# Within-chunk products of an S5 layer: formed on TensorE from zero-padded coefficients instead of gathered through DRAM

## The chip, the cores and the metric

One of the eight NeuronCores of a Trainium2 chip runs the whole program; the other seven are idle. The metric is device time of one execution in microseconds. Before the change three runs gave 2152.57, 2155.32 and 2158.06 us, median 2155.32. One further execution was profiled; it took 2160.6 us.

## The reference

Two layers of a hybrid encoder in float32, on 256 tokens of width 2048. Layer 0 mixes tokens with a bidirectional diagonal state-space model (S5), layer 1 with windowed attention; each is followed by a squared-ReLU MLP of width 8192. The change concerns the S5 mixer alone:

```
for each direction d (forward, backward), group g of 16 channels (128 groups, 64 states each):
    s[t] = lb[d,g] * s[t -/+ 1] + (f*B)[d,g] u[t]            # complex, over 256 tokens
    y[t] += Re(C[d,g] s[t])
y = y + d_skip * u ;  z = gelu(y)
h = h + (z @ w_glu_a) * sigmoid(z @ w_glu_b)
```

## The kernel before

The 256 tokens are cut into 64 chunks of T = 4. The recurrence runs over chunks only (63 steps); inside a chunk the answer is a product with a 64 x 64 matrix (4 tokens x 16 channels in and out) for each group. The 128 groups are handled in two halves of 64 ("half 0" and "half 1"), and each half in 8 batches of 8 groups, b = 0 to 7. A pair of batches, m = b // 2, shares one tile of products and one PSUM bank of outputs.

For one half the work is:

- `s5_a`: coefficient tables q (L469, VectorE for half 0, GpSimd for half 1), their transposes on TensorE (L477), and the state inputs of all chunks (L449).
- `s5_scan`: the recurrence, 63 steps of three VectorE instructions (L505, L506, L507).
- `s5_expand_steps`: the output tables E of a batch, on GpSimd (four L523 and two L524).
- `s5_kern`: the responses of a batch, B times E, eight matmuls on TensorE (L540), copied out by ScalarE (L547). `finish` adds the skip term on GpSimd (L553) and writes the responses to a DRAM scratch (L554, on SyncE's DMA queue).
- `s5_gather`: two DMAs (L564) read the scratch back with a shifted access pattern, and so form the product tile `tp` of a pair of batches, with zeros where a lag would be outside the chunk.
- `s5_shift`: state copies on ScalarE and VectorE (L582, L583), through a ring of two buffers. `s5_inner`: products times inputs into the output bank (L594). `s5_out`: states times E into the same bank (L607), then gelu. `s5_ztrans`: transposes of gelu's result (L619, L622, L623) into z.

Half 0's z opens the first part of the gated projection, `glu_early`: 32 weight tiles of 512 KB, loaded over ScalarE's queue, split in a high part (L638, ScalarE) and a low part (L639, VectorE or GpSimd), 12 matmuls of 128x512 each (L657 to L659). This work is in `run` placed between and around half 1's steps. The rest of the projection, the MLP, the attention and the second MLP follow; they take the larger part of the time and no step of theirs is edited.

The order on each engine comes from the tile framework's scheduler, which starts from the order of the program and moves instructions by its own estimate; each engine then executes its list strictly in order, and so do the DMA queues of SyncE and ScalarE.

Buffers are places in one arena of SBUF. A tile of half 1 often lies where a tile of half 0 was, so it must wait for that one's last reader: the tables E of half 1's batches 4 and 3 lie where those of half 0's batches 6 and 7 were, and those of batches 0 to 2 where half 0's inputs and states were.

Of the kernel before, what the change touches and what calls it, by code (L numbers as in the profile page):

```python
# [16 lines left out]
P = 128  # L17
# [14 lines left out]
PF = 1  # L32
SB, SC = 10, 2
ER, GM, GL, GA, GC = 0.3, 1, 2, 2, 6
# [132 lines left out]
class Kernel:  # L167
    def __init__(self, ctx, tc, d):
# [4 lines left out]
        self.dram = ctx.enter_context(tc.tile_pool(name="dram", bufs=8, space=bass.MemoryType.DRAM))  # L173
# [101 lines left out]
    def s5_setup(self):  # L275
# [11 lines left out]
        self.msk = ar.get("msk", [16], at=48128)  # L287
        self.dcol = ar.get("dcol", [32], at=48160)
        nc.scalar.dma_start(self.msk, d["dmask"])
        nc.scalar.dma_start(self.dcol, d["dcol"])  # L290
# [141 lines left out]
    def s5_a(self, h):  # L432
# [7 lines left out]
        def statein(b, pin):  # L440
            for i in range(0, 8, 4):
                bk = self.bank()
                for j in range(4):
                    gl = b * 8 + i + j
                    for ri in range(2):
                        for dr in range(2):
                            uu = u[:, gl // 2, gl % 2, :] if dr == 0 else u[:, gl // 2, gl % 2, ::-1]
                            c = (4 * ri + j) * NC
                            pe.matmul(bk[dr * H:(dr + 1) * H, c:c + NC],  # L449
                                      lhsT=pin[:, i + j, ri, dr * H:(dr + 1) * H], rhs=uu, start=True, stop=True)  # L450
# [7 lines left out]
        for b in range(8):  # L458
# [12 lines left out]
            pin = self.r_pin.next()  # L471
            for i in range(0, 8, 2):
                bk = self.bank()
# [4 lines left out]
                po = pin[:, i:i + 2].rearrange("p g r c -> p (g r c)")  # L478
# [4 lines left out]
                yield  # L483
            if prev is not None:
                if b == 1:
                    self.u_trans(h)
                    self.st.append(self.ar.get("st%d" % h, [NC, 2, 64], at=(31744, 23552)[h]))
                statein(*prev)
                yield
# [39 lines left out]
    def s5_kern(self, h, b):  # L529

        nc, d = self.nc, self.d
        g = nc.gpsimd
        u = h * 8 + b
        bp = self.r_bp.next()
        nc.sync.dma_start(bp, d["bp"][u])
        E = self.ex[h, b]
        bk = self.bank()
# [4 lines left out]
        md = self.r_md.next()  # L542
        mb = self.msk.rearrange("p (o c) -> p o c", o=1).broadcast_to([P, 2, 16])
        db = self.dcol[:, u * 2:u * 2 + 2].rearrange("p (g o) -> p g o", o=1).broadcast_to([P, 2, 16])
        g.tensor_mul(md, mb, db)
        kk = self.r_kk.next()
        self.kev = nc.scalar.copy(kk[:, :, 48:176], bk[:, :2 * P].rearrange("p (g c) -> p g c", g=2))  # L547
        if (h, b // 2) not in self.scr:
            self.scr[h, b // 2] = self.dram.tile([32, 4, 2, 448], F32, name="scr")
        scr = self.scr[h, b // 2]  # L550

        def finish():
            self.fin = g.tensor_add(kk[:, :, 48:64], kk[:, :, 48:64], md)  # L553
            nc.sync.dma_start(scr[:, :, b % 2].rearrange("r q c -> q r c"), kk.rearrange("p g c -> p (g c)"))  # L554
        return finish

    def s5_gather(self, h, m, at):

        tp = self.tp[h, m] = self.ar.get("tp%d%d" % (h, m), [16, 64], at=at)
        scr = self.scr[h, m].rearrange("p q x (s c) -> (p q x s) c", c=224)  # L560
        for dr in range(2):
            src = scr[dr * P * 2:(dr + 1) * P * 2, dr * 112:dr * 112 + 64]
            src = bass.AP(tensor=src.tensor, offset=src.offset, ap=[[16, T]] + [list(x) for x in src.ap])
            self.nc.sync.dma_start(tp[dr * 64:dr * 64 + 64].rearrange("p g c -> p (g c)"), src)  # L564

    def s5_kk(self, *ats):

        r = Ring([self.ar.get("kk#%d" % at, [2, 224], at=at) for at in ats])
        for kk in r.tiles:
            self.nc.gpsimd.memset(kk[:, :, 0:48], 0.0)  # L570
            self.nc.gpsimd.memset(kk[:, :, 176:224], 0.0)
        return r
# [12 lines left out]
    def s5_inner(self, h, m):  # L585
# [4 lines left out]
        for x in range(2):  # L590
            for j in range(8):
                i = j % 4 * 4 + x * 2 + j // 4
                c = (x * 4 + j // 2) * 64
                self.nc.tensor.matmul(y[j % 2 * H:(j % 2 + 1) * H, c:c + 64], lhsT=u[:, m * 8 + x * 4 + j // 2, j % 2, :], rhs=tp[:, i],  # L594
                                      start=(x == 0 and j < 2), stop=False, skip_group_check=True)
        self.ar.free("tp%d%d" % (h, m))

    def s5_out(self, h, b):
# [4 lines left out]
        for j in range(0, 8, 2):  # L603
            c = ((b % 2) * 4 + j // 2) * 64
            for n in range(2):
                for r in range(2):
                    pe.matmul(y[r * H:(r + 1) * H, c:c + 64], lhsT=so[:, j + r, n, :], rhs=E[:, j + r, n * T:(n + 1) * T, :], start=False,  # L607
# [539 lines left out]
    def run(self):  # L1147
# [11 lines left out]
        self.ex, self.tp, self.so, self.zt, self.scr, self.ybk = {}, {}, {}, {}, {}, {}  # L1159
        self.r_md = ar.ring("md", 2, [2, 16], at=48192)  # L1160
        self.r_q = ar.ring("q", 2, [8, 3, T, 16], at=4096)
        self.r_pin = ar.ring("pin", 2, [8, 2, P], at=7168)
        self.r_bca = ar.ring("bca", 2, [2, 8, 16], at=11264)
        self.r_bs = ar.ring("bs", 2, [8, 16], at=11776)
        self.r_bc = Ring([ar.get("bc#%d" % at, [2, 8, 2, 16], at=at) for at in (12032, 51712)])
        self.wt = ar.get("wt", [8, T, 16], at=48960)
        self.sct = ar.get("y", [2, 64], at=48704)
# [6 lines left out]
        self.r_bp = Ring([ar.get("bp#%d" % at, [8, 32], at=at) for at in (45568, 45824, 47104, 47360, 47616, 47872)])  # L1174
        self.r_kk = self.s5_kk(46080, 46592, 12544)
# [3 lines left out]
        att = dict(zip(KQ[0], (2048, 3072, 9216, 10240)))  # L1179
# [5 lines left out]
        last = []  # L1185

        def ekern(h, bs, n=0):

            wait = []
            for b in bs:  # L1190
                yield from expand(h, b)
                while last:
                    last.pop()()
                wait = [(m, k - 1) for m, k in wait]
                now = [x for x in wait if x[1] < 0 and (x[0] < 2 or "pin#0" not in ar.live)]
                for m, _ in now:
                    self.s5_gather(h, m, att[m])
                wait = [x for x in wait if x not in now]
                last.append(self.s5_kern(h, b))
                if h == 0 and b % 2:  # L1200
                    wait.append((b // 2, n))
                yield
            if h == 0:
                last.pop()()
                for m, _ in wait:
                    self.s5_gather(h, m, att[m])
        ek = ekern(0, order, 1)
# [3 lines left out]
        interleave(self.s5_a(1), (early(ek, 7 - PF), ER))  # L1211
        ar.free("bca", "bs", "q", "pin", "tab", "bc#12032")
        drain(ek)
        ar.free("kk#12544")
        del self.r_kk.tiles[2:]
        self.r_kk.i = 0
        self.r_bc.tiles[0] = ar.get("bc#12288", [2, 8, 2, 16], at=12288)
        drain(ekern(1, (7, 6, 5)))
        last.pop()()
        ar.free("kk", "bp")  # L1220
# [161 lines left out]
```

## Time and profile before

| | |
|---|---|
| median of three runs | 2155.32 us |
| profiled execution | 2160.6 us, of which its span is 2158.8 us |
| TensorE busy (matmul) | 2012.6 us, 93% |
| VectorE busy | 1247.7 us, 58% |
| ScalarE busy | 994.1 us, 46% |
| GpSimd busy | 337.6 us, 16% |
| mean granted TensorE clock | 0.972 |

The shares are means over very different stages. From 455 us to the end TensorE works almost without a pause; before about 345 us, the S5 mixer, no engine does. The profile page cuts the span into 40 slices, gives busy time by line, and follows back the chain of work that ended last; the trace can be asked for any window. In the rows below, PE is TensorE's matmuls, PEld its weight loads, DVE VectorE, ACT ScalarE, POOL GpSimd, SPq and ACTq the DMA issues of SyncE and ScalarE. An ordinary float32 matmul leaves two records in the trace and a transpose one: the eight matmuls of L540 show as x16.

### The profile page before, as it was taken

How to read it: one execution, taken by the hardware profiler on the slowest of the kernel's cores; microseconds unless marked ns; L12 is line 12 of the kernel's file. 1: busy time of each engine (PE TensorE's matmuls, PEld its weight loads, DVE VectorE, ACT ScalarE, POOL GpSimd, SP SyncE). 2: the span in 40 equal slices, each digit the busy share in tenths (PEclk: the TensorE clock that was granted, in tenths of full speed). 3: DMA queues.
4: the chain of work that ended last, by engine and by line, in shares of the span. 5: the costliest groups of instructions: out<-in, count | busy, mean ns of one | idle time of the engine just before them, and what ended most of it. 6: DMA issues, size and time to landing. Idle time of an engine off the chain costs nothing.

```text
span 2158.8 us, 29177 instructions
## 1 busy us (share of the span) xinstructions
PE 2012.6 (93%) x11860; PEld 1688.9 (78%) x11860; DVE 1247.7 (58%) x1820; ACT 994.1 (46%) x1233; POOL 337.6 (16%) x287
## 2 busy tenths in 40 slices
PE   2945879999999999999999889999999999999999
PEld 2834668878888888888888667788888888888887
DVE  6885924775555554444456777566555555444444
ACT  6734445444444444444444456554444444444442
POOL 6974952110000000000002432020000000000000
PEclk9976989999999999999999999999999999999999
DMA  2233555545555555565554332355555555555554
GB/s 96 59 80 110 174 155 206 184 167 194 187 187 183 192 180 196 193 214 195 201 195 156 127 137 98 118 194 186 195 183 189 195 190 182 202 190 194 194 194 156
DMA packets 78375, 368.49 MB, mean 171 GB/s; under 512 B 23473, under 2 KB 29905, under 8 KB 38305
## 3 DMA queue, kind: packets, MB, share of 16 engines
q1 hardware_dynamic: 72704, 346.78, 47.0%
q10 hardware_dynamic: 5328, 19.49, 2.8%
q8 instruction: 93, 1.52, 0.3%
q0 software_dynamic: 208, 0.36, 0.0%
q14 instruction: 42, 0.34, 0.0%
HBM read 360.83 MB, written 5.77 MB: 170 GB/s over the span
## 4 chain that ended last, share of the span: by engine, by line
PE 78%; DVE 7%; POOL 6%; DMA 5%; ACT 3%; issue 2%; SPq 0%; ACTq 0%; POOLq 0%; DVEq 0%
PE bank L849 32%; PE bank L798 22%; PE bank L799 11%; PE bank L657 3%; PE bank L659 3%; PE bank L658 3%; POOL slot L523 2%; POOL slot L524 1%; DMA scr<-slot 1%; DVE slot L639 1%; POOL slot L469 1%; DMA slot<-in_wge 1%; DVE slot L1014 1%; ACT slot L1010 1%; ACT slot L638 1%
## 5 line engine op out<-in xcount | busy, mean ns | idle before, releaser
L639 DVE TENSOR_TENSOR slot<-slot,slot 128x2048 fp32r<-128x2048 f32 (+1 forms) x321 | 713.2, 2225 | 729.4 <-ACT slot L638 725.5
L638 ACT CAST slot<-slot 128x2048 fp32r<-128x2048 f32 (+2 forms) x357 | 623.4, 1752 | 752.9 <-PE bank L849 364.6
L798 PE MATMUL bank<-slot,slot 128*128 128x512 f32 x2048 | 719.7, 397 | 0.0
L849 PE MATMUL bank<-slot,slot 128*128 128x512 f32 x3072 | 696.7, 389 | 0.0
L849 PEld LDWEIGHTS bank<-slot,slot 128*128 128x128 f32 x3072 | 576.6, 188 | 119.6
L799 PE MATMUL bank<-slot,slot 128*128 128x256 f32 x2048 | 571.7, 279 | 0.0
L798 PEld LDWEIGHTS bank<-slot,slot 128*128 128x128 f32 x2048 | 385.3, 188 | 92.2
L799 PEld LDWEIGHTS bank<-slot,slot 128*128 128x128 f32 x2048 | 386.9, 189 | 0.4
L657 PE MATMUL bank<-slot,slot 128*128 128x512 f32 x544 | 219.8, 405 | 2.3 <-ACT slot L638 1.2
L658 PE MATMUL bank<-slot,slot 128*128 128x512 f32 x544 | 216.4, 398 | 0.0
L659 PE MATMUL bank<-slot,slot 128*128 128x512 f32 x544 | 204.5, 399 | 6.4 <-POOL slot L639 5.4
L659 PEld LDWEIGHTS bank<-slot,slot 128*128 128x128 f32 x544 | 102.6, 191 | 30.1 <-POOL slot L639 6.7
L807 ACT ACTIVATE slot<-slot 128x256 f32<-128x256 f32 x128 | 53.5, 420 | 156.8 <-DVE slot L806 156.8
L657 PEld LDWEIGHTS bank<-slot,slot 128*128 128x128 f32 x544 | 104.9, 193 | 26.4 <-ACT slot L638 1.6
L658 PEld LDWEIGHTS bank<-slot,slot 128*128 128x128 f32 x544 | 104.8, 193 | 21.6 <-issue 0.7
L639 POOL TENSOR_TENSOR slot<-slot,slot 128x1024 fp32r<-128x1024 f32 (+2 forms) x36 | 99.6, 2779 | 99.7 <-ACT slot L638 76.9
L920 POOL DMA_DIRECT2D slot<-in_pos x1 | 0.8, 754 | 611.9 <-DVE slot L842 611.9
L540 PE MATMUL bank<-slot,slot 128*32 128x128 f32 x256 | 13.6, 346 | 54.1 <-POOL slot L524 54.1
L477 PE MATMUL bank<-ident,slot 128*128 128x128 f32 x256 | 42.0, 327 | 21.6 <-DVE slot L469 16.4
L505 DVE TENSOR_TENSOR bank<-bank,slot 128x256 f32<-128x256 f32 x126 | 54.4, 432 | 6.6 <-ACT slot L456 2.4
L806 DVE SCALAR_TENSOR_TENSOR slot<-slot 128x256 f32<-128x256 f32 x128 | 54.2, 425 | 4.2
L477 PEld LDWEIGHTS bank<-ident,slot 128*128 128x128 f32 x256 | 35.8, 169 | 25.7 <-POOL slot L411 16.4
(212 smaller groups left out, 1413.3 us busy)
## 6 DMA issues: line engine op xcount, KB each, us to landing
slot<-in_wup SPq DMA_DIRECT2D x128, 1024.0 KB
slot<-in_wdn SPq DMA_DIRECT2D x128, 1024.0 KB
slot<-in_wqkv SPq DMA_DIRECT2D x20, 1024.0 KB
slot<-in_wge ACTq DMA_DIRECT2D x32, 512.0 KB
slot<-in_wgl SPq DMA_DIRECT2D x16, 1024.0 KB
slot<-in_wo SPq DMA_DIRECT2D x16, 1024.0 KB
slot<-in_cp SPq DMA_DIRECT2D x16, 256.0 KB
slot<-scr SPq DMA_DIRECT2D x16, 256.0 KB
```

The lines of the kernel that those rows point to most:

```text
L477: pe.transpose(bk[:, (2 * j + ri) * P:(2 * j + ri + 1) * P], qf[:, ri * H:ri * H + P], self.ident)
L505: yield v.tensor_mul(xy, lb, st[:, k - 1].rearrange("p r (o g) -> p r o g", o=1).broadcast_to([P, 2, 2, n]))
L638: self.nc.scalar.copy(hi[:, c], raw[:, c])
L639: (self.nc.gpsimd if e == "g" else self.nc.vector).tensor_sub(lo[:, c], raw[:, c], hi[:, c].bitcast(F32))
L657: pe.matmul(out, lhsT=xh, rhs=wh, start=first, stop=False)
L658: pe.matmul(out, lhsT=xl, rhs=wh, start=False, stop=False)
L659: pe.matmul(out, lhsT=xh, rhs=wl, start=False, stop=last)
L798: pe.matmul(bk, lhsT=wh[:, kt], rhs=act[:, kt].rearrange("p x c -> p (x c)"), start=(kt == 0), stop=False)
L799: pe.matmul(bk[:, :L], lhsT=wl[:, kt], rhs=act[:, kt, 0], start=False, stop=(kt == KT - 1))
L806: nc.vector.scalar_tensor_tensor(s, s, 0.0, rb, op0=ALU.max, op1=ALU.mult)
L807: nc.scalar.activation(hT(fb), s, AF.Square)
L849: pe.matmul(bks[tt][cb], lhsT=x[:, ts], rhs=w[:, cb * 512:(cb + 1) * 512], start=(kt == 0 and w is wh and x is hh), stop=(kt == NK - 1 and ...
```

## The change

- The products within chunks are now made by TensorE itself. For a batch, B is stored with 16 zero columns before its 16 real ones (`bz`, 128x672, with the skip coefficients behind), so a 32-column weight slice that starts 16 columns earlier or later lands the 16 real rows in the upper or lower half of a 32-partition quadrant, and adds zeros to the other half. 70 matmuls with 32 weight columns and 16 to 256 moving columns add the responses of the right lags to one PSUM bank; the last four add the skip term. One ScalarE copy of 128x512 puts the bank into `tp`.
- The DRAM scratch, its writes and gathers, the `kk` buffers and their memsets, and the skip term on GpSimd (L545, L553) are gone. The load per batch grows from 128x256 to 128x672 values.
- Half 0's first two `s5_inner` run as soon as their products exist, during `s5_a` of half 1; the other two right after the eighth batch.
- Half 1's tables and products for batches 7, 6, 5 and 4 are placed between half 0's outputs (`EK`), where before 7, 6 and 5 came ahead of all of half 0's outputs; batches 3, 0, 1, 2 follow among the weight tiles of the projection.
- `s5_a`: the transposed tables are in halves of 4 groups in a ring of 3 instead of 8 groups in a ring of 2, and the state inputs of the batch before are issued in the middle of a batch.
- Scan of half 1: `SB, SC` from 10, 2 to 0, 1 (steps issued between half 0's outputs). Some buffers move.

```diff
-SB, SC = 10, 2
-ER, GM, GL, GA, GC = 0.3, 1, 2, 2, 6
+PF, EE, ER = 1, 6, 0.3
+SB, SC = 0, 1
+EK = {1: 7, 3: 6, 5: 5, 6: 4}
+GM, GL, GA, GC = 1, 2, 3, 6
...
-    def s5_kern(self, h, b):
...
-        for j in range(8):
-            q, c = j % 4, j // 4 * P
-            nc.tensor.matmul(bk[q * 32:(q + 1) * 32, c:c + P], lhsT=bp[:, j],
-                             rhs=E[:, j].rearrange("p s c -> p (s c)"), start=True, stop=True)
...
-        def finish():
-            self.fin = g.tensor_add(kk[:, :, 48:64], kk[:, :, 48:64], md)
-            nc.sync.dma_start(scr[:, :, b % 2].rearrange("r q c -> q r c"), kk.rearrange("p g c -> p (g c)"))
-        return finish
-
-    def s5_gather(self, h, m, at):
...
-            self.nc.sync.dma_start(tp[dr * 64:dr * 64 + 64].rearrange("p g c -> p (g c)"), src)
...
+        w = bz[:, :544]
+        sk = bz[:, 544:672].rearrange("p (g c) -> p g c", g=8)
+
+        def mm(q, g, t, lhsT, rhs, start=False, stop=False):
+            self.km = nc.tensor.matmul(o[q * 32:(q + 1) * 32, g, t], lhsT=lhsT, rhs=rhs, start=start, stop=stop, skip_group_check=True)
+        al = slice(0, 8)
+        for q, t in ((0, slice(0, 2)), (3, slice(2, T))):
+            mm(q, al, t, w[:, 512:544], E[:, :, 0:2], start=True)
+        for g in range(8):
+            for k in range(2):
+                for q in range(4):
+                    dr, jj = q // 2, q % 2 * 2 + (k if q % 2 == 0 else 1 - k)
+                    tk = T - 1 - jj
+                    t, lag = (slice(tk, T), slice(0, T - tk)) if dr == 0 else (slice(0, tk + 1), slice(2 * T - 1 - tk, 2 * T))
+                    c = (g * 2 + dr) * 32 + (0 if jj % 2 else 16)
+                    mm(q, g, t, w[:, c:c + 32], E[:, g, lag], start=(g == 0 and k == 0 and q in (1, 2)), stop=(g == 7 and k == 1 and dr == 1))
+        for k in range(2):
+            for q in range(2):
+                tk = T - 1 - (q * 2 + k)
+                c = 0 if k else 16
+                mm(q, al, tk, self.irep[:, c:c + 32], sk, stop=(k == 1))
+        x = b % 2 * 8
+        self.kev = nc.scalar.copy(self.tp[h, m][:, x:x + 8].rearrange("p g c -> p (g c)"), bk)
...
+            if i in EK:
+                drain(expand(1, EK[i]))
+                with self.tc.issue_after(self.om.ins):
+                    self.s5_kern(1, EK[i], att[1][EK[i] // 2])
...
-        for b, m, at in ((4, 3, 50688), (3, 2, 49664), (0, None, 0), (1, None, 0), (2, 0, 2048)):
-            finish = self.s5_kern(1, b)
-            glu(1)
-            finish()
-            if m is not None:
-                self.s5_gather(1, m, at)
+        for b in (3, 0, 1, 2):
+            self.s5_kern(1, b, att[1][b // 2])
             glu(GA)
```

TensorE's list before, from the last state inputs of half 1 to half 0's first outputs (L540 responses of a batch, L594 inner products, L607 outputs, L619 transposes of z; slots are places in the arena, and slot_191 as weights marks half 1's batches here):

```order
L449 MATMUL bank<-slot_85,slot_191 64x64 x64
L540 MATMUL bank<-slot_75,slot_73 32x128 x8
L540 MATMUL bank<-slot_191,slot_73 32x128 x24
L594 MATMUL bank<-slot_75,slot_84 64x64 x19
L607 MATMUL bank<-slot_78,slot_75 64x64 x32
L594 MATMUL bank<-slot_75,slot_84 64x64 x13
L607 MATMUL bank<-slot_87,slot_75 64x64 x16
L619 MATMUL bank<-ident,slot_75 128x128 x4
```

The same place now (L447 state inputs, L544 the new products of a batch, of which the first rows stand here, L583 inner products, L596 outputs, L608 transposes of z):

```order
L447 MATMUL bank<-slot_82,slot_188 64x64 x32
L544 MATMUL bank<-slot_73,slot_79 32x8x32 x2
L544 MATMUL bank<-slot_73,slot_79 32x16
L544 MATMUL bank<-slot_73,slot_79 32x64 x2
...
L544 MATMUL bank<-slot_71,slot_79 32x8x16 x4
L583 MATMUL bank<-slot_188,slot_81 64x64 x32
L596 MATMUL bank<-slot_76,slot_73 64x64 x32
L544 MATMUL bank<-slot_188,slot_79 32x8x32 x2
...
L544 MATMUL bank<-slot_79 32x8x16 x4
L596 MATMUL bank<-slot_84,slot_73 64x64 x16
L608 MATMUL bank<-ident,slot_73 128x128 x4
```

Three batches of half 1 (the x24) stood ahead of half 0's inner products and outputs; now only half 0's last two batches (140 matmuls) stand there, and half 1's batches stand after the first two, the fourth and the sixth output.

SyncE's DMA list before, at half 1's first batches among the projection's weights (in_cp and in_bp are a batch's coefficients, scr the scratch):

```order
L514 DMA slot_191<-in_cp 128x512
L554 DMA scr<-slot_75 4x32x448
L535 DMA slot_191<-in_bp 128x256
L514 DMA slot_86<-in_cp 128x512
L554 DMA scr<-slot_84 4x32x448
L564 DMA slot_86<-scr 64x16x64 x2
L535 DMA slot_191<-in_bp 128x256
L554 DMA scr<-slot_75 4x32x448
L554 DMA scr<-slot_84 4x32x448
```

The last coefficient loads now, up to the projection's second kind of weights (in_wgl):

```order
L534 DMA slot_79<-in_bz 128x672
L534 DMA slot_188<-in_bz 128x672
L534 DMA slot_79<-in_bz 128x672
L514 DMA slot_73<-in_cp 128x512
L514 DMA slot_83<-in_cp 128x512
L534 DMA slot_188<-in_bz 128x672
L534 DMA slot_79<-in_bz 128x672
L514 DMA slot_73<-in_cp 128x512
L534 DMA slot_188<-in_bz 128x672
L622 DMA slot_82<-in_wgl 128x2048 x2
```

Every wait on a scratch write or read has left this queue; what it still waits for is buffers, of which `bz` has five for half 0 and two for half 1.

## Rows read from the trace of the kernel before

**Rows 1.** The profile page, first line.

```profile
span 2158.8 us, 29177 instructions
```

**Rows 2.** Windows: stretch, length; PE, PEld, DVE, ACT, POOL busy; PEclk; DMA share; GB/s.

```profile
79.00:153.00 74.00, 48.78 (x816) 42.70 (x811) 64.61 (x189) 43.64 (x69) 61.21 (x78) 0.84 0.28 74
153.00:181.00 28.00, 3.47 (x54) 2.08 (x56) 8.26 (x15) 0.74 (x2) 20.89 (x23) 0.54 0.35 87
181.00:212.00 31.00, 20.96 (x399) 18.88 (x396) 25.24 (x52) 25.38 (x28) 10.15 (x11) 0.78 0.32 104
212.00:318.00 106.00, 86.11 (x515) 67.23 (x515) 64.45 (x162) 43.39 (x52) 81.35 (x52) 0.89 0.55 161
318.00:345.00 27.00, 27.00 (x339) 22.49 (x337) 10.74 (x11) 17.99 (x19) 9.55 (x4) 0.98 0.66 235
455.00:2158.00 1703.00, 1680.23 (x8605) 1410.76 (x8603) 939.73 (x1199) 764.69 (x934) 82.93 (x43) 0.99 0.52 181
```

**Rows 3.** Chain that ended last, 136 to 185 us: start, length, what.

```profile
172.27 9.01 DMA scr<-slot
...
183.81 1.22 PE bank L607 x17
```

**Rows 4.** The same chain, 264 to 345 us.

```profile
281.94 0.23 PE bank L658
...
291.53 12.83 DMA scr<-slot
...
304.94 10.97 DMA slot<-scr
...
318.03 1.42 PE bank L607 x32
```

**Rows 5.** Waits, 140 to 320 us: who for whom, total us, times, longest.

```profile
ACT slot L547 <- DMA scr<-slot: 20.3, 2, 15.1
POOL slot L523 <- DMA slot<-in_cp: 17.3, 6, 5.5
```

**Rows 6.** Timeline of PE: start, length, line, shape, records merged.

```profile
57.94 1.97 PE L477 MATMUL bank<-ident,slot 128*128 128x128 f32 x16
...
67.66 2.08 PE L449 MATMUL bank<-slot,slot 128*64 128x64 f32 x64
...
79.36 0.64 PE L540 MATMUL bank<-slot,slot 128*32 128x128 f32 x16
...
90.08 3.76 PE L329 MATMUL bank<-ident,slot 128*128 128x128 f32 x32
...
183.81 1.97 PE L607 MATMUL bank<-slot,slot 128*64 128x64 f32 x32 [0.50 <-ACT slot L583]
...
193.26 1.10 PE L594 MATMUL bank<-slot,slot 128*64 128x64 f32 x32
```

**Rows 7.** Window of dense small matmuls, columns as in rows 2.

```profile
60.00:80.00 20.00, 20.00 (x465) 18.79 (x464) 16.32 (x24) 11.74 (x16) 17.30 (x19) 1.00 0.23 62
```

**Rows 8.** Timeline of VectorE: half 0's last step is over, two steps of half 1.

```profile
153.27 0.84 DVE L582 COPY slot<-slot 64x504 f32<-64x504 f32 x1
...
239.25 0.43 DVE L505 TENSOR_TENSOR bank<-bank,slot 128x256 f32<-128x256 f32 x1
...
267.19 0.43 DVE L505 TENSOR_TENSOR bank<-bank,slot 128x256 f32<-128x256 f32 x1
```

**Rows 9.** VectorE by line, 79 to 318 us: count, busy us, mean ns, idle before.

```profile
L639 DVE TENSOR_TENSOR slot<-slot,slot 128x1024 fp32r<-128x1024 f32 x8 | 13.6, 1696 | 1.1 <-ACT slot L638 1.0
L582 DVE COPY slot<-slot 64x504 f32<-64x504 f32 x12 | 10.0, 837 | 48.1 <-PE bank L607 47.8
```

**Rows 10.** GpSimd by line, 0 to 345 us, columns as in rows 9.

```profile
L524 POOL TENSOR_TENSOR slot<-slot,slot 128x512 f32<-128x512 f32 x32 | 44.5, 1391 | 0.5
L523 POOL TENSOR_TENSOR slot<-slot 128x512 f32<-128x512 f32 x32 | 36.6, 1155 | 12.5 <-DMA slot<-in_cp 11.1 <-PE bank L607 1.0
...
L469 POOL TENSOR_TENSOR slot<-slot,slot 128x512 f32<-128x512 f32 x24 | 26.3, 1130 | 0.0
```

More of the change, by code (lines that the diff above doesn't have):

```diff
@@ L470, in s5_a @@
                 yield
-            pin = self.r_pin.next()
+            pin = [self.r_pin.next(), None]
             for i in range(0, 8, 2):
+                if i == 4:
+                    if prev is not None:
+                        if b == 1:
+                            self.u_trans(h)
+                            self.st.append(self.ar.get("st%d" % h, [NC, 2, 64], at=(31744, 23552)[h]))
+                        statein(*prev)
+                        yield
+                    pin[1] = self.r_pin.next()
                 bk = self.bank()
@@ L482, in s5_a @@
                     self.evac = a.copy(po, bk)
[L483 to L488, printed above, removed]
                 yield
@@ L527, in s5_expand, with s5_kern @@
         drain(self.s5_expand_steps(*a))
-    def s5_kern(self, h, b):
[L531 to L535, printed above, removed]
+    def s5_kern(self, h, b, at=None):
+        nc = self.nc
+        u, m = h * 8 + b, b // 2
+        bz = self.r_bz.next()
+        nc.sync.dma_start(bz, self.d["bz"][u])
         E = self.ex[h, b]
+        if (h, m) not in self.tp:
+            self.tp[h, m] = self.ar.get("tp%d%d" % (h, m), [16, 64], at=at)
@@ L1184, in run, with ekern @@
         q = [self.s5_scan(0)]
-        last = []
-        def ekern(h, bs, n=0):
-            wait = []
+        def ekern(h, *bs):
             for b in bs:
                 yield from expand(h, b)
[L1192 to L1201, printed above, removed]
-                yield
[L1203 to L1207, printed above, removed]
+                self.s5_kern(h, b, att[h][b // 2])
+                if b in (1, 3):
+                    self.s5_inner(0, b // 2)
+                yield
+        ek = ekern(0, *order)
         steps(ek, 3 * PF)
@@ L1210, in run @@
         q.append(self.s5_scan(1))
[L1211 to L1212 removed]
+        interleave(self.s5_a(1), (early(ek, EE - PF), ER))
+        ar.free("bca", "bs", "q", "pin", "tab")
         drain(ek)
[L1214 to L1220, printed above, removed]
[L1221 to L1222 removed]
+        ar.free("bc#12032")
+        self.r_bc.tiles[1] = ar.get("bc#6656", [2, 8, 2, 16], at=6656)
+        self.r_bc.i = 1
         def sc(n):
@@ L1231, in run @@
             g.memset(so[:, :, 1, NC - 1:NC], 0.0)
+        for m in range(2, 4):
+            self.s5_inner(0, m)
+        ar.free("bz#45568", "bz#46240", "bz#46912")
+        del self.r_bz.tiles[2:]
+        self.r_bz.i = 0
         prev = None
-        kev = self.kev
         for i, b in enumerate(order):
-            if i % 2 == 0:
-                self.s5_inner(0, b // 2)
-            with self.tc.issue_after(kev.ins):
-                self.s5_shift(0, b, v.tensor_copy)
+            self.s5_shift(0, b, v.tensor_copy)
             self.s5_out(0, b)
```

80 lines of the change are left out of this document (27 added, 53 removed).

## The prediction

> **What bounds the kernel now.** I read the windows first, then the chain, then the waits and single engines. The windows show where TensorE, which carries the program, pauses [rows 2]. From 455 us on it is busy 1680 of 1703 us, and from 318 to 345 us 27 of 27: whatever starts earlier there ends earlier, one for one. Ahead of that it is busy 48.8 of 74 us (79 to 153), 3.5 of 28 (153 to 181), 21.0 of 31 (181 to 212) and 86.1 of 106 (212 to 318): 79.6 of 239 us are idle, and the granted clock falls to 0.54 in the emptiest stretch. The reader should see that no engine is full between 153 and 181 us: VectorE has 8.3 us, ScalarE 0.7, GpSimd 20.9.
>
> The chain says why. At 172.27 a scratch write of 9.0 us ends a wait of ScalarE, whose queue holds the response copies of half 1's batches ahead of half 0's state copies; half 0's outputs start at 183.81 [rows 3], though its recurrence was over at 153.27 [rows 8]. At the other end, 12.8 us of scratch write and 11.0 us of gather follow one another, and half 1's outputs start at 318.03 [rows 4]. The waits show the same queue from two sides: ScalarE's response copy waits 20.3 us for scratch writes, and GpSimd's tables 17.3 us for coefficient loads, which stand behind those writes on SyncE [rows 5].
>
> **The change part by part.** *Scratch, gathers, GpSimd's skip term.* They go, with all waits on them. What is late next is TensorE, because it takes the work over.
>
> *Price of a batch on TensorE.* A batch was eight matmuls, 16 records, 0.64 us [rows 6]. Now it is 70 matmuls, 140 records, 3584 moving columns against 1024. No row shows 16 to 48 moving columns on 32 weight columns. By columns it would be 3.5 x 0.64 = 2.2 us; by records of that row 140 x 0.040 = 5.6 us; by the 64-column records, 2.08 us for 64 and 1.10 for 32, it is 140 x 0.0325 = 4.55 us. At the lower clock the same kind of record took 1.97 / 32 = 0.062 us [rows 6], so 8.6 us a batch. Below 2.2 us I see no reason to go. I take 4.55, as most of the new matmuls have 16 to 64 columns and those rows are nearest, and full clock, because a stretch full of such matmuls was granted 1.00 [rows 7].
>
> What those rows show is about 33 ns a record at 64 columns, whether 64 are needed or fewer. The Trainium skill (TensorEngine Tiling (Array Packing), Instruction Overhead) says that a matmul carries about 60 cycles whatever it streams, so that one column costs as much as 60, and advises against cutting a dimension that is already small. It speaks against this change: as an estimate, 140 times 25 ns is 3.5 us a batch, not 2.2. By the page the sum below would be about 2112 us, by the rows 2125.
>
> *Start of half 0's outputs.* TensorE's list from the end of half 0's state inputs, 79.4 us: half 1's 128 transposes, 1.97 / 16 each, 15.8; its 512 state-input records, 0.0325 each, 16.6; 32 input transposes 3.8; four inner products, 128 records at 0.034, 4.4; eight batches at 4.55, 36.4 [rows 6]. Together 77.0, so 156.4 us without a wait, where before there were 48.8 us of work in 74. VectorE gives nearly the same: its recurrence of half 0 is not touched and ends at 153.3, and four state copies of 0.84 bring it to 156.6 [rows 8, 9]. GpSimd is earlier than both: its eight tables are 8 x (4 x 1.155 + 2 x 1.391) = 59 us and the 24 coefficient products 27 us [rows 10], as before, but without up to 17.3 us of waits. I add 3.5 us for waits of TensorE on tables and on ScalarE's copies: 160 instead of 183.8, **24 us earlier**.
>
> *From there to half 1's first output.* TensorE's list: half 0's 256 output records at 0.034, 8.7; 16 transposes of z, 2.0; 240 weight matmuls at 0.23 [rows 4], 55.2; eight batches, 36.4; half 1's first inner product 1.1. That is 103.4, so 263.4. To this I add 16 us of waits. Eight are for half 0's outputs, which ScalarE paces: 25.4 of 31 us in that stretch before, with TensorE at 21.0 [rows 2]; three new batches fill only part of it. Five are a new wait: the first matmuls of half 1's batch 4 now stand ahead of z's last transposes, and table 4 lies where half 0's table 6 was, so GpSimd can only finish it (about 6 us, two products and two sums left [rows 10]) once half 0's outputs are through. Behind it TensorE's whole list waits, the first weight matmul included. Three are for cold stretches. So 279.4 against 318.0, **38.6 us earlier**, the 24 of the first part among them.
>
> The other engines must allow it. VectorE after 153.3: 63 steps at (267.19 - 239.25) / 25 = 1.118, 70.4; 16 state copies, 13.4; eight low parts, 13.6; with a few us for z it is free at about 254 [rows 8, 9], 25 us before 279. GpSimd: tables 4, 3, 0, 1, 2 from about 188, 37 us, to 225; its first low part belongs to the ninth weight tile, which TensorE reaches after 96 weight matmuls and four to five batches, at about 233.
>
> *Given back.* Counted in the order of TensorE's list, 276 weight matmuls stood ahead of half 1's first output, now 240: 36 x 0.23 = **8.3 us** later.
>
> *Sum.* 38.6 - 8.3 = 30.3. The profiled execution took 2160.6 us (its span of 2158.8 [rows 1] and 1.8 around it), so 2130 for one like it. It lies 5.3 us above the median of the runs, 2155.3; the forecast for the median is **2125 us**.
>
> The regrouped transposes of `s5_a` and the wider coefficient loads I cost at nothing: the former issue the same instructions, the latter are covered by five buffers in half 0. In half 1 there are two, so a load waits for the batch two before it; if that shows, it is the third rival.
>
> **The rivals.** *The price of the small matmuls decides (slower).* TensorE now has nearly no slack, and 16 batches are on its path. Each us of a batch costs up to 16; the gain is gone at 4.55 + 30 / 16 = 6.4 us, 46 ns a record. At the lower clock's 8.6 us the time is 2125 + 16 x 4.05 = 2190. For it: the clock was 0.84 from 79 to 153 and 0.54 afterwards [rows 2], and TensorE waits for each table in list order, which leaves pauses. Against it: those clocks belong to an engine idle for a third of the time and more, and the dense stretch had 1.00 [rows 7].
>
> *Cheaper.* If a record costs 16 to 25 ns, TensorE loses up to 2.3 us x 8 in the second part, but the first stays with VectorE at about 158 and the second cannot pass VectorE's 254 and half 1's state copies: first output at about 262, time 2125 - 17 = 2108. The page's 3.5 us belongs here.
>
> *A new wait on VectorE.* Its list holds 85 instructions of half 1's recurrence, some 28 steps or 31.7 us [rows 8], behind the eighth low part, whose buffer (one of three) is freed by the fifth weight tile's matmuls. I expect that at 214 to 222. If it slips past 247, each us is lost again; 15 late is 2140. For it: in-order lists that cross three engines; against: 25 us of slack.
>
> *The waits change their name only.* Half 0's first products need tables, loads and ScalarE copies in turn; if half 0's outputs still start at about 180, 20 of the 30 us stay away: 2145 to 2155. For it: the recurrences, the tables and ScalarE's copies are untouched. Against it: in the rows of 153 to 181 us only the scratch queue is late.
>
> **How the numbers follow.** Forecast 0.50, for 2113 to 2138 (its own range: 1.6 us a batch less or more in the second part, or half of the waits). Cheaper 0.16, for 2104 to 2113. VectorE's wait 0.10, for 2138 to 2149. Waits renamed 0.14, half of it within 0.3% of 2155.3 (2148.8 to 2161.8, about what a measurement of this kernel can tell from no change) and half below. Slower 0.10, of which 0.03 is within 0.3%. So faster 0.83, same 0.10, slower 0.07. The range that leaves out 2 in 10 is 2106 to 2150: the row price of 5.6 us a batch, 2142, lies in it, the lower clock's price does not.
>
> **What the profile after would show.** No scratch DMA. L544 in 16 groups of 140 records, each 3.5 to 5.6 us long; longer groups make the first rival. Half 0's first L596 at about 160 (153 to 168), half 1's first L596 at about 279 (262 to 292). TensorE over 85% busy from 79 to 153 and at a clock above 0.95. TensorE waiting for GpSimd's table 4 for some us just before the first weight matmul. VectorE's last L507 some 20 us ahead of half 1's first output; if it comes right before it, the third rival holds. The forecast is wrong in its core if half 0's outputs start after 175, or if TensorE's busy time before half 1's outputs grows by over 90 us.

## The result and the profile after

The changed kernel takes 2126.68 us (median of four runs, 2125.68 to 2131.74) against 2156.36 us before: ratio 0.9869, 95% interval 0.9849 to 0.9890, or 29.7 us faster. The forecast was 2125 us. The profiled execution took 2126.57 us (span 2124.8), 34.0 us under the one of before. Eight runs of the changed kernel lie in two groups, four at 2125.7 to 2126.8 and four at 2131.4 to 2131.9 us, whose profiled executions agree up to half 1's last output (299.4 and 299.0 us) and differ in the second MLP, whose first product (L787) takes 356.4 us in one and 362.8 in the other, so differences under 5 us are read from marks in the traces below, not from medians.

The windows after the change, to be laid beside [rows 2] (same columns):

```profile
79.00:153.00 74.00, 63.06 (x1926) 55.20 (x1924) 67.44 (x192) 47.37 (x71) 69.70 (x72) 0.98 0.28 80
153.00:181.00 28.00, 21.51 (x607) 18.27 (x605) 26.14 (x60) 22.47 (x25) 8.43 (x7) 0.70 0.20 65
181.00:212.00 31.00, 24.85 (x424) 19.71 (x417) 29.46 (x60) 6.07 (x9) 26.87 (x20) 0.88 0.47 145
212.00:318.00 106.00, 102.93 (x1158) 82.17 (x1157) 65.22 (x119) 60.31 (x68) 71.24 (x34) 1.00 0.49 163
```

TensorE's idle time from 79 to 318 us falls from 79.7 to 26.7 us, so its busy time grows by 53.0. The empty stretch from 153 to 181 us, 3.5 us of work before, now has 21.5, at a granted clock of 0.70 against 0.54. From 212 to 318 us the clock is 1.00.

TensorE's timeline of the changed kernel at the places the prediction named (start, length, line, shape, records merged, and in brackets the idle time before and what ended it):

```profile
78.47 2.55 PE L544 MATMUL bank<-slot,slot 128*32 128x256 f32 x140
...
151.59 0.34 PE L596 MATMUL bank<-slot,slot 128*64 128x64 f32 x4 [1.99 <-ACT slot L572]
...
157.32 3.58 PE L544 MATMUL bank<-slot,slot 128*32 128x256 f32 x125
...
171.25 0.48 PE L596 MATMUL bank<-slot,slot 128*64 128x64 f32 x4 [4.26 <-DVE slot L572]
...
183.38 1.04 PE L596 MATMUL bank<-slot 128*64 128x64 f32 x28 [0.25 <-DVE slot L573]
188.41 1.14 PE L544 MATMUL bank<-slot,slot 128*32 128x256 f32 x8 [3.99 <-POOL slot L524]
...
192.54 0.78 PE L646 MATMUL bank<-slot,slot 128*128 128x512 f32 x1
...
265.94 1.15 PE L596 MATMUL bank<-slot,slot 128*64 128x64 f32 x31
...
298.24 1.15 PE L596 MATMUL bank<-slot,slot 128*64 128x64 f32 x32
```

A batch of 140 records takes 2.55 us at full clock and about 4.3 at the low one (the row at 157.32 is its first 125 records; the clock granted from 157.3 to 161.5 us was 0.56). Half 0's outputs (L596) run from 151.6 to 184.4 us; there is a wait of 4.26 us for a state copy on VectorE and the foreseen one of 3.99 us for GpSimd's table 4. The first weight matmul (L646) comes at 192.5, half 1's first output at 265.9. The marks in the kernel before, from the same view:

```profile
212.08 0.78 PE L657 MATMUL bank<-slot,slot 128*128 128x512 f32 x1
...
300.21 1.10 PE L607 MATMUL bank<-slot,slot 128*64 128x64 f32 x32
304.19 1.15 PE L607 MATMUL bank<-slot,slot 128*64 128x64 f32 x32
316.05 1.97 PE L594 MATMUL bank<-slot,slot 128*64 128x64 f32 x32 [7.77 <-DMA slot<-scr]
317.79 1.66 PE L607 MATMUL bank<-slot,slot 128*64 128x64 f32 x32
...
341.65 1.15 PE L607 MATMUL bank<-slot,slot 128*64 128x64 f32 x32
```

Here half 1's outputs start at 300.2, not at 318.0: the chain in [rows 4] passes through the third of the eight outputs, the one behind the last gather. With equal marks the gain adds up so (36 weight matmuls fewer stand ahead of half 1's outputs, 36 x 0.228 = 8.2 us):

| mark | before | after | earlier | less the 36 |
|---|---|---|---|---|
| first weight matmul | 212.1 | 192.5 | 19.5 | 19.5 |
| half 1's first output | 300.2 | 265.9 | 34.3 | 26.1 |
| half 1's last output begins | 341.7 | 298.2 | 43.4 | 35.2 |
| end | 2158.8 | 2124.8 | 34.0 | 34.0 |

So I read 19.5 us as the scratch route's waits in half 0 and the pauses around its outputs, 6.6 as waits between there and half 1's outputs, and 9.1 as the wait for the last gather and the records at the lower clock behind it. TensorE's own costliest wait before the change, from 79 to 184 us, names another engine (who for whom, total us, times, longest):

```profile
PE bank L540 <- POOL slot L524: 44.6, 6, 11.5
```

These are GpSimd's tables, which for a part of that time waited for coefficient loads behind the scratch writes [rows 5]. No run takes the scratch route alone out of the kernel before; what the place of the tables is worth without it is the second experiment.

### The profile page after: what moved, and what is told of

Read it like the earlier page. It is cut to its first block, busy times and chain, and to the rows that moved or that the text cites. A ratio compares the mean times of both kernels' runs of the same rounds, so it can differ in the third digit from the quotient of the medians.

```text
span 2124.8 us, 33046 instructions
## 1 busy us (share of the span) xinstructions
PE 2034.0 (96%) x13844; PEld 1706.7 (80%) x13844; DVE 1255.5 (59%) x1820; ACT 996.3 (47%) x1233; POOL 334.5 (16%) x245
## 3 DMA queue, kind: packets, MB, share of 16 engines
q8 instruction: 108, 1.77, 0.3%
## 4 chain that ended last, share of the span: by engine, by line
PE 73%; DVE 4%; ACT 2%; DMA 2%; issue 1%; POOL 0%; SPq 0%; ACTq 0%; DVEq 0%
PE bank L838 32%; PE bank L787 22%; PE bank L788 11%; PE bank L646 2%; PE bank L647 2%; PE bank L648 2%; DVE slot L628 1%; ACT slot L999 1%; DMA slot<-in_wqkv 1%; ACT slot L627 1%; DVE slot L1003 1%; PE bank L1018 1%; PE bank L1009 1%; DVE slot L984 1%; DMA slot<-in_wup 0%
## 5 line engine op out<-in xcount | busy, mean ns | idle before, releaser
L787 PE MATMUL bank<-slot,slot 128*128 128x512 f32 x2048 | 719.5, 397 | 0.0
L787 PEld LDWEIGHTS bank<-slot,slot 128*128 128x128 f32 x2048 | 385.3, 188 | 92.0
L646 PE MATMUL bank<-slot,slot 128*128 128x512 f32 x544 | 218.4, 403 | 6.2 <-ACT slot L627 5.1
L646 PEld LDWEIGHTS bank<-slot,slot 128*128 128x128 f32 x544 | 103.7, 191 | 30.8 <-ACT slot L627 6.5
L483 PE MATMUL bank<-ident,slot 128*128 128x128 f32 x256 | 37.2, 295 | 22.3 <-DVE slot L467 16.0
L664 POOL TENSOR_TENSOR slot<-slot 128x512 f32<-128x512 f32 x16 | 28.9, 1813 | 171.6 <-DVE slot L1117 62.5
L830 ACT CAST slot<-slot 128x256 fp32r<-128x256 f32 x128 | 50.7, 397 | 8.0 <-PE bank L838 7.9
```

What stands on the lines that cost most here:

```text
L646: pe.matmul(out, lhsT=xh, rhs=wh, start=first, stop=False)
L787: pe.matmul(bk, lhsT=wh[:, kt], rhs=act[:, kt].rearrange("p x c -> p (x c)"), start=(kt == 0), stop=False)
L830: nc.scalar.copy(hh, hT(kt))
```

## The experiments

The ratios are to the kernel before, with 95% intervals.

| run | median, us | ratio |
|---|---|---|
| after_again | 2131.60 | 0.9883 (0.9870 to 0.9896) |
| half1_ahead | 2127.08 | 0.9868 (0.9856 to 0.9881) |
| x2_half0 | 2137.16 | 0.9916 (0.9903 to 0.9929) |
| x2_half1_late | 2144.63 | 0.9953 (0.9937 to 0.9970) |
| tables_swapped | 2121.75 | 0.9842 (0.9829 to 0.9855) |
| no_steps_between | 2126.27 | 0.9866 (0.9853 to 0.9880) |
| swap_sc0 | 2127.38 | 0.9874 (0.9857 to 0.9890) |
| scan1_half | 2128.47 | 0.9875 (0.9858 to 0.9892) |
| one_group_at_a_time | 2150.06 | 0.9964 (0.9951 to 0.9976) |
| x2_spread | 2135.21 | 0.9903 (0.9881 to 0.9925) |
| more_weights_ahead | 2129.35 | 0.9869 (0.9854 to 0.9883) |
| swap_sc0_weights | 2117.12 | 0.9814 (0.9795 to 0.9833) |

### Which part of the change is worth something

The changed kernel again, as a base on the same chip:

> The changed kernel as it is, beside the others, so that they have one on the same chip. All theories: 2126 to 2132 us, ratio 0.985 to 0.989 to the kernel before; half 0's first L596 at about 152 us, half 1's at about 266.

Its median is 2131.60 us; the marks are those above (151.5, 192.5, 265.5 us). Then the placement alone undone:

```diff
+        for b in (7, 6, 5):
+            drain(expand(1, b))
+            self.s5_kern(1, b, att[1][b // 2])
         prev = None
         for i, b in enumerate(order):
...
-EK = {1: 7, 3: 6, 5: 5, 6: 4}
+EK = {6: 4}
```

> The products stay on TensorE, only the placement is undone: tables 7, 6 and 5 of half 1 and their products stand ahead of half 0's outputs again, as in the kernel before. My theory (both parts give something, the products more): half 0's outputs wait for GpSimd's three tables, which ended at about 158 us in the changed kernel, and begin at 160 to 163 instead of 152; part of it comes back, because the outputs no longer have three batches between them. 5 to 10 us slower than the changed kernel, 2132 to 2137. Rival, the placement is the gain: 20 us slower or more, 2147 and above. Rival, the placement is worth nothing, because state copies pace the outputs anyway: within 2 us of the changed kernel.

My theory failed: the time is that of the changed kernel. TensorE's timeline:

```profile
163.69 0.45 PE L596 MATMUL bank<-slot,slot 128*64 128x64 f32 x8
...
185.98 1.04 PE L596 MATMUL bank<-slot 128*64 128x64 f32 x28 [1.05 <-DVE slot L573]
...
194.35 0.78 PE L646 MATMUL bank<-slot,slot 128*128 128x512 f32 x1
...
298.53 1.15 PE L596 MATMUL bank<-slot,slot 128*64 128x64 f32 x32
```

Half 0's outputs start 12.1 us later than in the changed kernel but end 2.6 later; the first weight matmul is 1.8 later, half 1's last output 0.3. Half 0's outputs take 33 us when they start early and 23 when they start late, with the three batches already done. So the placement of half 1's tables between the outputs is worth nothing measurable here; the gain is that of the products on TensorE and of the parts that came with them. The regrouped `s5_a`, half 0's early inner products, `SB, SC` and the moved buffers were not undone one by one, so their shares stay open. Of the 32 us by which half 0's outputs start earlier only about 20 reach the next mark.

### What a batch costs, and where it is hidden

```diff
         al = slice(0, 8)
+        for _ in range(2 if h == 0 else 1):
...
```

The loop goes around all 70 matmuls of a batch, which are issued again into the same bank.

> Each of half 0's eight batches is formed twice in the same bank (560 more matmuls, 1120 records, 8 x 2.3 to 2.5 = 18 to 20 us more of TensorE). My theory: part of it lies beside VectorE's recurrence of half 0, which ends at about 149 us; TensorE was idle for 10.9 of the 74 us from 79 to 153, so 8 to 10 us come through, 2135 to 2138, with half 0's first L596 at 160 to 162. Rival, the batches are on the path everywhere, as the prediction's sum had it: 18 to 20 us slower, 2145 to 2148. Rival, VectorE alone sets half 0's start: within 3 us of the changed kernel.

Measured 2137.16 us: 5.6 to 10.5 more, the expected part of some 20 us added, but not by the expected way. The mark was missed: half 0's first output came at 177.5 instead of 160 to 162, because TensorE also paused for 20.6 us (all pauses from 75 to 345 us put down to "issue"; 4.5 in the changed kernel). By the first weight matmul, 209.1, 16.6 us are left of the delay, and at the first matmul of the MLP (407.0 us in the changed kernel) 15.5. Of these 4.8 return in the first MLP, which the edit does not touch: in the 25 us from its start TensorE waits 4.1 us for GpSimd in the changed kernel, at a granted clock of 0.86, and 1.6 us here, at 1.00. So some 15 us come through the mixer, more than the theory had, and the time met the forecast because a later wait became shorter.

The same for the batches behind half 0's outputs:

```diff
+        for _ in range(2 if h == 1 and b < 5 else 1):
```

> The five batches of half 1 that stand behind half 0's outputs (4, 3, 0, 1, 2) are formed twice: 5 x 2.3 to 2.5 = 11.5 to 12.5 us more of TensorE between 188 and 240 us. My theory: TensorE is full from 192 to 300 us, so all of it comes through: 11 to 13 us slower than the changed kernel, 2138 to 2141, half 1's first L596 at 277 to 279. Rival, VectorE's recurrence of half 1 (over at 256) or its state copies hold half 1's outputs: under 4 us slower.

Measured 2144.63 us, 13 to 18 more; half 1's first output at 288.5, 22.6 us later, more than my theory had (4.5 of them return in the first MLP as above). Nothing hides batches there, and a doubled batch costs 4.5 us, not 2.5. TensorE's timeline shows why:

```profile
222.67 4.25 PE L544 MATMUL bank<-slot,slot 128*32 128x256 f32 x260
228.97 0.73 PE L544 MATMUL bank<-slot,slot 128*32 128x64 f32 x20 [2.05 <-issue]
...
255.71 4.29 PE L544 MATMUL bank<-slot,slot 128*32 128x256 f32 x267
261.85 0.65 PE L544 MATMUL bank<-slot,slot 128*32 128x48 f32 x13 [1.85 <-issue]
```

After some 260 short records in a row TensorE stops for 2 us with nothing to wait for. The DMA view of 226 to 227 us in the same kernel (queue, packets, MB, share):

```profile
q8 instruction: 1, 0.02, 6.0%
```

One packet of the instruction queue starts in this window, at 226.7 us, and takes 1.0 us, so it lands 1.3 us ahead of the resumption at 228.97; others start at 241.9 and 259.4 us and land 1.4 and 1.5 us ahead of the resumptions at 244.32 and 261.85. (39 such packets come from 75 to 345 us, most of them with no pause behind.) That would be the stream of instructions falling behind; two more edits take this and the price itself apart.

```diff
-        for g in range(8):
-            for k in range(2):
-                for q in range(4):
+        for q in range(4):
+            for g in range(8):
+                for k in range(2):
```

> The 64 short matmuls of each batch are issued one 32-column group after the other (q as the outer loop) instead of in turn over the four groups; same matmuls, same columns. My theory (a record takes some 200 ns from start to end and only records of different column groups run side by side, so that 140 records start 16 ns apart in the changed kernel): the groups of L544 get longer, 4 us or more instead of 2.55 at full clock, and the time rises by 5 us or more. Rival (a record starts every 16 ns whatever group it is on): L544 stays at 2.5 to 2.6 us and the time stays within 2 us of the changed kernel.

```profile
78.49 5.70 PE L544 MATMUL bank<-slot,slot 128*32 128x256 f32 x140
...
103.49 5.70 PE L544 MATMUL bank<-slot,slot 128*32 128x256 f32 x140
```

The theory's price holds: the same 70 matmuls take 5.70 us instead of 2.55 when neighbours write the same 32 output partitions, 41 ns a record instead of 16 to 18. Its word "only" does not. The single records of the first batch start 31 to 32 ns apart within a group at 16 and 32 moving columns, 42 to 43 at 48 and 55 to 56 at 64, and each lasts 180 to 220 ns, so records of one group overlap too. These distances are the same whether the next matmul adds to columns of the bank just written (the next k) or to others (the next g), so it is not the adding to the same place that costs. The Trainium skill (TensorEngine Tiling (Array Packing), Key Properties) says that different tiles of the array can execute their weight loads and matmuls in parallel; the trace agrees, 2.55 against 5.70 us. TensorE is busy in 74.0 of the 74 us from 79 to 153, its pauses for issue shrink to 0.6 us, and the time is 2150.06: with this loop order 7 us under the kernel before of the same comparison (2157.15) would be left, of the 24 to 30 us that the changed kernel gains.

Then the doubled batch with weight matmuls between the two:

```diff
             self.s5_kern(1, b, att[1][b // 2])
-            glu(GA)
+            glu(1)
+            self.s5_kern(1, b, att[1][b // 2])
+            glu(GA - 1)
```

> Batches 3, 0, 1, 2 of half 1 are formed twice as before, but with 12 weight matmuls between the two (4 more loads of coefficients and 4 more copies of ScalarE come with it). When the two stood back to back, five doubled batches moved half 1's first L596 from 266 to 288 us, 4.5 us each, with pauses of 1.2 to 2.8 us after some 260 short records in a row, and a 16 KB packet of the instruction queue landing in each. My theory (the stream of instructions can't follow such long rows of short records; single batches ride on what is already there): now 2.6 to 3.2 us each, half 1's first L596 at 276 to 279, and pauses of TensorE put down to issue of 7 us at most before it (13.9 in the doubled kernel, 4.5 in the changed one). Rival (a repeated batch costs 4.5 us because of the repetition itself, writing the bank again): first L596 at 283 or later.

Half 1's first output came at 280.2, 14.3 us later for four batches: between theory and rival (time 2135.21 us; 4.8 us return in the first MLP). The pauses stay at 4.6 us (13.9 back to back), so they go with the length of the dense run, not with the repetition. TensorE's waits from 79 to 280 us show what else there is (line, what for, us in total, times, longest):

```profile
PE bank L544 <- issue: 4.6, 5, 1.3
...
PE bank L544 <- ACT slot L562: 2.9, 1, 2.9
PE bank L544 <- DMA slot<-in_bz: 0.2, 1, 0.2
```

Without these 3.1 us, which the second copy and load bring, it is 2.8 us a batch. That late instructions cause the pauses fits all of these rows; it is not proved by them, as the trace shows no wait for an instruction.

### Who paces half 0's outputs

Half 0's tables placed otherwise, so that half 1's table 4 finds its place free after the fourth output:

```diff
-        at0 = dict(zip(order, (13312, 14336, 16384, 17408, 15360, 18432, 0, 1024)))
+        at0 = dict(zip(order, (13312, 14336, 1024, 0, 15360, 18432, 17408, 16384)))
```

> Half 0's tables 2 and 3 trade places with 7 and 6, so that half 1's table 4 lies where a table is free after the fourth output instead of the seventh. My theory (the wait on table 4 and the transposes of z queued behind it hold the first weight matmul): TensorE no longer waits 2 to 4 us for GpSimd before z's transposes, the first weight matmul comes at 187 to 189 us instead of 192.5, the time is 3 to 5 us under the changed kernel. Rival, the wait only changes its name (Gelu, state copies): first weight matmul within 1 us of 192.5, time the same.

About 5 us faster than the changed kernel (four of five runs at 2120.2 to 2121.8 us). The trace is of the fifth run, 2129.69 us, and serves for marks in the mixer only: it is 3.2 us ahead of the changed kernel's trace up to the second MLP and loses 6.4 us there, in an unedited stage. The first weight matmul is at 190.6, not 187 to 189, but batch 4 is now done ahead of it, and half 1's last output, with 324 weight matmuls ahead of it in both traces, begins 5.5 us earlier, at 292.8:

```profile
292.78 1.15 PE L596 MATMUL bank<-slot,slot 128*64 128x64 f32 x32
```

The wait on table 4, with what queued behind it, was real.

No recurrence step of half 1 between half 0's outputs:

```diff
-SB, SC = 0, 1
+SB, SC = 0, 0
```

> No step of half 1's recurrence is put between half 0's outputs in the program (one per batch before). My theory (VectorE's list, with up to 19 recurrence instructions ahead of a state copy, paces half 0's outputs): the last of these outputs ends at 175 to 179 us instead of 184.4, the first weight matmul comes at 184 to 188. Half 1's recurrence then ends later than 256, at 258 to 266; up to there it is hidden. Time 2 to 6 us under the changed kernel. Rival, VectorE's recurrence of half 1 is what half 1's outputs wait for: half 1's first output not earlier than 266, time the same or up to 5 us longer.

Both sides of the expectation came true in part. In TensorE's timeline the outputs end at 176.6 us and the first weight matmul is 8.5 us earlier, but half 1's first output is 3.8 later. The scheduler has put 48 more weight matmuls ahead of that output (288 instead of 240), so the equal mark is the last output, with 324 ahead of it in both: it begins at 296.5, 1.8 us earlier:

```profile
175.57 1.03 PE L596 MATMUL bank<-slot 128*64 128x64 f32 x28 [0.80 <-ACT slot L573]
...
184.06 0.78 PE L646 MATMUL bank<-slot,slot 128*128 128x512 f32 x1
...
269.69 0.34 PE L596 MATMUL bank<-slot,slot 128*64 128x64 f32 x4 [1.20 <-ACT slot L572]
...
296.47 1.15 PE L596 MATMUL bank<-slot,slot 128*64 128x64 f32 x32
```

The recurrence's last line by source, in the changed kernel and in this one (count; duration min/median/max; first and last start):

```profile
L507 DVE TENSOR_TENSOR slot<-bank,slot x126: 277/291/293, 80.6 to 256.1; 128x128 f32<-128x128 f32 x126
```

```profile
L507 DVE TENSOR_TENSOR slot<-bank,slot x126: 284/291/294, 80.3 to 267.7; 128x128 f32<-128x128 f32 x126
```

The recurrence ends 11.6 us later and half 1's outputs start right behind it, with waits for their state copies: from 260 to 300 us TensorE is idle for 4.3 us, at a granted clock of 0.87, where in the changed kernel it is idle for none, at 1.00. VectorE's list is the limit one step behind TensorE's: most of a pause taken out of half 0's outputs comes back between half 1's. The median, 2126.27 us, is that of the changed kernel. Both edits together:

```diff
-SB, SC = 0, 1
+SB, SC = 0, 0
...
-        at0 = dict(zip(order, (13312, 14336, 16384, 17408, 15360, 18432, 0, 1024)))
+        at0 = dict(zip(order, (13312, 14336, 1024, 0, 15360, 18432, 17408, 16384)))
```

> Both edits: tables traded and no recurrence step between half 0's outputs. My theory: the gains add, first weight matmul at 180 to 184 us, half 1's first output at 256 to 260, time 5 to 9 us under the changed kernel. Rival, VectorE's total work from 150 us on (70 us of steps, 14 of copies, 14 of low parts) is the bound: half 1's first output not before 262, time 0 to 4 us under it.

The rival held: the first weight matmul is at 184.4, but half 1's recurrence now ends at 277.1 (its last step is read by no copy), and its first output waits:

```profile
276.00 0.48 PE L596 MATMUL bank<-slot,slot 128*64 128x64 f32 x4 [6.09 <-ACT slot L572]
```

Half of half 1's recurrence left out:

```diff
-        for k in range(1, NC):
+        for k in range(1, NC if h == 0 else NC // 2):
```

> Leaves out the last 32 of half 1's 63 recurrence steps (36 us of VectorE); everything else stays. My theory (VectorE matters only where steps stand ahead of half 0's state copies; later TensorE is full): first weight matmul 0 to 5 us earlier than 192.5, time 0 to 6 us under the changed kernel. Rival, VectorE is the bound between half 0's outputs and half 1's: 10 us or more under it.

No change (2128.47 us, first weight matmul at 193.0, half 1's first output at 267.2 though the recurrence was over at 211.4). In the changed kernel VectorE is 10 us ahead of half 1's outputs and TensorE's list holds them; the steps that stand ahead of half 0's state copies belong to the half that stayed.

### What was "given back", and a faster version

```diff
-GM, GL, GA, GC = 1, 2, 3, 6
+GM, GL, GA, GC = 1, 2, 3, 9
```

> 36 more weight matmuls ahead of half 1's outputs (GC 9 instead of 6), as many as the kernel before had. The prediction's sum counted these 36 as 8.3 us given back. My theory (they are only moved; TensorE is full there, so it is a shift of the mark, not of the end): half 1's first L596 at 273 to 275 us instead of 266, the time within 2.5 us of the changed kernel. Rival (what stands ahead of half 1's outputs is late for good): 6 to 8 us slower.

Half 1's last output begins 9.2 us later (307.4), the first only at 267.9 instead of 273 to 275, as the scheduler put the new weights among the first outputs. The time, 2129.35 us, lies inside the range of the changed kernel's runs (2125.7 to 2131.9). Weights ahead of half 1's outputs move the mark by 9.2 us, of which 3.0 are left at the first matmul of the MLP in this trace (410.0 instead of 407.0): less than the 6 to 8 of the rival, though not shown to be nothing.

So such weights can cover the later end of the recurrence. On top of the two edits of the run that traded the tables and put no step between:

```diff
-GM, GL, GA, GC = 1, 2, 3, 6
+GM, GL, GA, GC = 1, 2, 3, 10
```

> Tables traded, no recurrence step between half 0's outputs, and 48 more weight matmuls ahead of half 1's outputs, to cover the later end of half 1's recurrence (277 us). My theory: first weight matmul at 184 to 186, TensorE no longer waits for half 1's state copies (9 us in the kernel without these weights), time 2117 to 2121, the fastest so far. Rival, VectorE stays the bound and the wait only moves behind the weights: 2124 to 2128.

```profile
183.25 0.47 PE L646 MATMUL bank<-slot,slot 128*128 128x512 f32 x1
...
277.95 2.20 PE L596 MATMUL bank<-slot,slot 128*64 128x64 f32 x64
```

The first weight matmul is 9.3 us earlier than in the changed kernel, and the first output no longer waits for its state copy. 2117.12 us, 0.9814 of before: the fastest median, with an interval that lies under those of the changed kernel and slightly overlaps that of the run that only trades the tables (0.9829 to 0.9855).

## Why the prediction was right, and where it was not

The time was right to 2 us (4 by the middle of all eight runs, 2129.1), the mechanism too; but two terms of the sum were wrong and cancelled in part, so that this closeness is luck. From profile to profile the forecast was 30.3 us and 34.0 came.

*Price of a batch: mis-sized.* Forecast 4.55 us, measured 2.55 at full clock and 4.3 at the low clock; the 16 batches carry 46.8 us of TensorE's busy time, 2.9 each. The 33 ns a record were read from records with 64 weight columns and 64 moving ones; no row showed four 32-column groups in turn, and none showed fewer columns, so "or fewer" was not in those rows. The range of 2.2 to 5.6 us held, and both orders lie near its ends: 2.55 in turn, 5.70 one group after the other. The sum for 5.6 us, 2142, was 8 under what this price did (2150), which is about the error of the mark below. The 3.5 us estimated from the Trainium skill (TensorEngine Tiling (Array Packing), Instruction Overhead) lie between the two orders and describe neither; the measurements decide. The 2112 us put beside them do not follow from the prediction's own prices: eight batches at 1.05 us less give 2117.

*The mark of half 1's outputs: misread.* "38.6 us earlier" compares half 1's first output after the change (279.4) with the third one before (318.0). At equal marks it was 300.2 to 279.4, plus the 9.1 us that, as measured, vanish between the first output and the last, or 29.9 us, and after the 8.3 given back 21.6 instead of 30.3. With the right mark my own prices gave 2134 us. Half 1's outputs then came 13.5 us earlier than I had them. 8.4 of these were there at half 0's first output (151.6 instead of 160); 5.1 arose from there on (columns as in [rows 2]):

```profile
151.59:265.88 114.29, 99.75 (x1664) 80.08 (x1666) 98.11 (x222) 57.98 (x67) 81.11 (x50) 0.90 0.42 130
```

TensorE's batches took 24.9 us of this stretch instead of 36.4, but the rest of its list 74.9 instead of 67.0, because records at the lower clock are longer (0.74 granted from 151.6 to 192.5 us; 28 output records took 1.76 us at 0.50 and 1.04 at 1.00), for which I had 3 us among the waits. The mark made the forecast 9 us too early, the price and the start 13 too late.

*The rival "cheaper" is what happened*, as a mechanism: a record at 16 to 18 ns, half 1's first output at 265.9 (forecast for it 262), VectorE 10 us ahead instead of 25 (256.1; forecast 254). Its time of 2108 started from the same wrong mark; from 2134 it would have been 2117.

*Half 0's outputs 24 us earlier*: 32 in fact. I had read 153.27 as the end of half 0's recurrence. VectorE was through with the steps that its copies read at 149.9; then it waited for ScalarE's copy of half 1's state inputs, and half 0's first state copy stood behind that in its list. Before, and after the change:

```profile
152.80 0.43 DVE L505 TENSOR_TENSOR bank<-bank,slot 128x256 f32<-128x256 f32 x1 [2.44 <-ACT slot L456]
```

```profile
149.53 1.21 DVE L572 COPY slot<-slot 64x504 f32<-64x504 f32 x1
```

The copies now start at 149.5, and TensorE was ready. The step's weak point was that it passed this on one for one: the outputs are paced, and an output start 12 us later changed nothing.

*Waits of 16 us* between half 0's first and half 1's first output: 14.5 in the stretch above. Table 4 was put at 5 us (the two products and two sums of [rows 10] are 5.1, not about 6); the wait is 4.0, and taking it away gave about 5.

*36 weights, 8.3 us given back*: right as bookkeeping between marks; by themselves they cost some 3 us or less.

*The other rivals.* VectorE's eighth low part came at 216.5 us (forecast 214 to 222) and held nothing up; that VectorE is the next bound is shown by the recurrence, not by it. The waits did not merely change names. That small matmuls could make the change nearly worthless is true for a batch written in the other loop order, with 7 us left.

*The signs named beforehand*: TensorE 85% busy from 79 to 153 at 0.98, the wait for table 4, 53 us more busy time, half 1's first output inside 262 to 292: seen. L544 at 3.5 to 5.6 us and half 0's first output at 153 to 168: missed on the quick side.

## What to carry to other kernels

Matmuls on 32-column groups should be issued in turn over the groups: here that is a factor of 2.2 in their price, and three quarters of the gain. Compare two traces at marks with the same work behind them, the first of its kind with the first, and subtract what was only moved past the mark. A stage that starts earlier is worth what its end gains; look for the mark from which the bounding engine is full, and ask which engine's list stands one step behind it.

## What was not expected of the hardware

Short records come at 16 to 18 ns each for some 260 in a row, then TensorE pauses for 1.2 to 2.8 us, with 16 KB packets of the instruction queue (108 of them, 1.77 MB, in the changed kernel) landing shortly before it goes on (1.3 to 1.5 us in the three pauses looked at); that they cause the pauses is not shown. Most single batches of 140 records between slower matmuls are free of this, two in a row are not; at 41 ns a record the pauses shrink to 0.6 us in all.
